# Loads and stores of 512 KB, one for each 128-token tile, in place of 2 MB for each group of 512 tokens

## The chip, the core and the metric

The kernel runs on one core of a Trainium2 chip. Its engines used here: TensorE (PE; its weight loads are shown as PEld), ScalarE (ACT), VectorE (DVE), GpSimd (POOL, only for constants) and SyncE (SP), which issues the loads and stores. All transfers run on the core's 16 DMA engines. The metric is device time in microseconds (us), median of several runs.

## The reference

Each of 64 x 1024 tokens has 1024 features, seen as 16 heads of 64. A product with `route_w` gives 16 logits per token; the head with the largest logit is the token's. Each head has its own 64 x 64 matrix. The output of a token is zero but in its best head, where it is that head's features times that head's matrix.

```python
route_logits = x @ route_w                       # x: 64 x 1024 x 1024, route_w: 1024 x 16
best_head = np.argmax(route_logits, axis=-1)
x_heads = x.reshape(B, S, H, Dh)                 # H = 16, Dh = 64
for h in range(H):
    mask = (best_head == h)
    transformed = np.matmul(x_heads[:, :, h, :], experts[h])
    out[:, :, h, :] = transformed * mask[:, :, None]
```

All is float32; x is 268 MB, and so is the output.

## The kernel before

The 65,536 tokens are cut into 128 groups of 512, and a group into T = 4 tiles of 128 tokens. The program is written out in full, without loops on the chip. `load(g)` (line 83) brings a group with one transfer of 2 MB: partition p gets four tokens that follow each other in memory, 16 KB in one piece, and tile t is the t-th of the four. Four such buffers (`XIN_BUFS`) are 64 KB of each partition, and as much again are the four output buffers.

For each tile, `transpose_tile` turns eight blocks of 128 features by matmuls with the identity (line 93), four to a PSUM buffer, and ACT copies each four to `xt` (line 94). When four tiles are in `xt`, `route` computes the logits of the 512 tokens in 16 matmuls (line 103) in four column strips; ACT copies the result (line 107), four matmuls turn it (line 110), and six DVE instructions (lines 112 to 124) make the mask of 0 and 1. `expert_tile` has 64 small matmuls for a tile (line 133: 8 pairs of heads, two halves of features, two halves of tokens), and DVE multiplies by the mask into `ot` (line 138).

The main loop (line 145) works on two groups at once: the transposes of group g alternate, tile by tile, with the expert matmuls of group g-1. The store of group g-1 (line 157) is one transfer of 2 MB after its fourth tile. In all there are 32 transposes, 256 expert matmuls, 16 + 4 matmuls of the route for a group, 308, and each has a weight load of its own. PE works in order.

SP issues loads and stores from one queue in a fixed order, and an instruction that waits holds all behind it. A load waits until PE has turned the group that used its buffer; a store waits for DVE's fourth multiplication. Transfers signal their end on eight semaphores in turn, and a transfer also waits for the one that used its semaphore before. The expert matrices (`ew`) and `route_w` (`rw`) come once, at the start, in rows of 256 and 64 bytes, issued by ACT.

Of the kernel before, what the change touches and what calls it, by code (L numbers as in the profile page):

```python
# [8 lines left out]
FP32 = mybir.dt.float32  # L9
# [3 lines left out]

P = 128
T = 4
XIN_BUFS = 4
OUT_BUFS = 4
XT_BUFS = 2


@with_exitstack
def kernel(
    ctx: ExitStack,
    tc: tile.TileContext,
    x: bass.AP,
    route_w: bass.AP,
    experts: bass.AP,
    out: bass.AP,
):

    nc = tc.nc
    B, S, D = x.shape
    H = experts.shape[0]
    Dh = D // H  # L40
    N = B * S
    NB = D // P
    G = T * P
    NG = N // G
    CG = 4
    CW = P // CG
    assert D % P == 0 and N % G == 0 and Dh * H == D and 2 * Dh == P and NB % CG == 0

    xg = x.rearrange("b s d -> (b s) d").rearrange("(g p t) d -> g p t d", p=P, t=T)
    og = out.rearrange("b s d -> (b s) d").rearrange("(g p t) d -> g p t d", p=P, t=T)  # L50

    consts = ctx.enter_context(tc.tile_pool(name="consts", bufs=1))
    small = ctx.enter_context(tc.tile_pool(name="small", bufs=2))
    xin_pool = ctx.enter_context(tc.tile_pool(name="xin", bufs=XIN_BUFS))
    xt_pool = ctx.enter_context(tc.tile_pool(name="xt", bufs=XT_BUFS))
    out_pool = ctx.enter_context(tc.tile_pool(name="outp", bufs=OUT_BUFS))
    ps_t_pool = ctx.enter_context(tc.tile_pool(name="ps_t", bufs=2, space=bass.MemoryType.PSUM))
    ps_e_pool = ctx.enter_context(tc.tile_pool(name="ps_e", bufs=2, space=bass.MemoryType.PSUM))
    ps_r_pool = ctx.enter_context(tc.tile_pool(name="ps_r", bufs=1, space=bass.MemoryType.PSUM))
    ps_l_pool = ctx.enter_context(tc.tile_pool(name="ps_l", bufs=1, space=bass.MemoryType.PSUM))  # L60

    ident = consts.tile([P, P], FP32, name="ident")
    make_identity(nc, ident)


    ew = consts.tile([P, NB, Dh], FP32, name="ew")
    ev = experts.rearrange("(p two) d e -> two d p e", two=2)
    for half in range(2):
        nc.scalar.dma_start(out=ew[half * Dh:(half + 1) * Dh, :, :], in_=ev[half])


    rw = consts.tile([P, NB, CW], FP32, name="rw")
    nc.vector.memset(rw, 0.0)  # L73
    with nc.allow_non_contiguous_dma(reason="route_w rows of 64 bytes, once"):
        nc.scalar.dma_start(out=rw[:, :, 0:H], in_=route_w.rearrange("(p k) h -> k p h", k=P))


    rank_i = consts.tile([P, T, H], I32, name="rank_i")
    nc.gpsimd.iota(rank_i, pattern=[[0, T], [-1, H]], base=H, channel_multiplier=0)
    rank = consts.tile([P, T, H], FP32, name="rank")  # L80
    nc.vector.tensor_copy(out=rank, in_=rank_i)  # L81

    def load(g):
        xin = xin_pool.tile([P, T, D], FP32, name="xin", tag="xin")
        nc.sync.dma_start(out=xin, in_=xg[g])
        return xin

    def transpose_tile(xin, xt, t):
        for half in range(2):
            ps_t = ps_t_pool.tile([P, NB // 2, P], FP32, name="ps_t", tag="ps_t")  # L90
            for q in range(NB // 2):
                p = half * (NB // 2) + q
                nc.tensor.transpose(ps_t[:, q, :], xin[:, t, p * P:(p + 1) * P], ident)  # L93
            nc.scalar.copy(  # L94
                out=xt[:, half * (NB // 2):(half + 1) * (NB // 2), t * P:(t + 1) * P],
                in_=ps_t)

    def route(xt):
        ps_r = ps_r_pool.tile([P, G], FP32, name="ps_r", tag="ps_r")
        for r in range(NB // CG):  # L100
            for c in range(CG):
                p = r * CG + c
                nc.tensor.matmul(  # L103
                    ps_r[c * CW:(c + 1) * CW, :], lhsT=rw[:, p, :], rhs=xt[:, p, :],
                    start=(r == 0), stop=(r == NB // CG - 1))
        lgt = small.tile([P, G], FP32, name="lgt", tag="lgt")
        nc.scalar.copy(out=lgt, in_=ps_r)  # L107
        ps_l = ps_l_pool.tile([P, T, P], FP32, name="ps_l", tag="ps_l")
        for t in range(T):
            nc.tensor.transpose(ps_l[:, t, :], lgt[:, t * P:(t + 1) * P], ident)  # L110
        lg = small.tile([P, T, H], FP32, name="lg", tag="lg")
        nc.vector.tensor_reduce(  # L112
            out=lg, in_=ps_l.rearrange("k t (c h) -> k t h c", c=CG)[:, :, 0:H, :],
            op=ALU.add, axis=AX.X)
        mx = small.tile([P, T], FP32, name="mx", tag="mx")
        nc.vector.reduce_max(out=mx, in_=lg, axis=AX.X)  # L116
        hit = small.tile([P, T, H], FP32, name="hit", tag="hit")
        nc.vector.tensor_tensor(  # L118
            out=hit, in0=lg, in1=mx.unsqueeze(2).to_broadcast([P, T, H]), op=ALU.is_ge)
        nc.vector.tensor_tensor(out=hit, in0=hit, in1=rank, op=ALU.mult)  # L120
        top = small.tile([P, T], FP32, name="top", tag="top")
        nc.vector.reduce_max(out=top, in_=hit, axis=AX.X)  # L122
        mask = small.tile([P, T, H], FP32, name="mask", tag="mask")
        nc.vector.tensor_tensor(  # L124
            out=mask, in0=hit, in1=top.unsqueeze(2).to_broadcast([P, T, H]), op=ALU.is_equal)
        return mask

    def expert_tile(xt, mask, ot, t):
        ps_e = ps_e_pool.tile([P, 2, NB, Dh], FP32, name="ps_e", tag="ps_e")
        for p in range(NB):  # L130
            for half in range(2):
                for th in range(2):
                    nc.tensor.matmul(  # L133
                        ps_e[th * 64:(th + 1) * 64, half, p, :],
                        lhsT=xt[half * 64:(half + 1) * 64, p, t * P + th * 64:t * P + (th + 1) * 64],
                        rhs=ew[half * 64:(half + 1) * 64, p, :],
                        start=True, stop=True)
        nc.vector.tensor_tensor(  # L138
            out=ot[:, t, :].rearrange("k (p two e) -> k two p e", two=2, e=Dh),
            in0=ps_e,  # L140
            in1=mask[:, t, :].rearrange("k (p two) -> k two p", two=2).unsqueeze(3).to_broadcast([P, 2, NB, Dh]),
            op=ALU.mult)

    prev = None
    for g in range(NG + 1):
        if g < NG:
            xin = load(g)
            xt = xt_pool.tile([P, NB, G], FP32, name="xt", tag="xt")
        if prev is not None:
            ot = out_pool.tile([P, T, D], FP32, name="ot", tag="ot")  # L150
        for t in range(T):
            if g < NG:
                transpose_tile(xin, xt, t)
            if prev is not None:
                expert_tile(prev[0], prev[1], ot, t)
        if prev is not None:
            nc.sync.dma_start(out=og[g - 1], in_=ot)
        prev = (xt, route(xt)) if g < NG else None


# [28 lines left out]
```

## Time and profile before

| | |
|---|---|
| median of 2 runs | 1873.62 us (1869.89 to 1877.36) |
| profiled execution, its own time | 1866.91 us |
| its span, first to last instruction | 1865.0 us |
| mean granted TensorE clock | 0.926 |
| busy: PE, DVE, ACT | 84%, 44%, 34% |
| HBM read, written | 268.76 MB, 268.44 MB |
| DMA queue of x and out (q1) | 36,864 packets, 76.2% of 16 engines' span |

The page lists, for one execution, how long each engine was busy, which chain of work ended last, and how much each DMA queue moved. "issue" in a chain or a wait is time in which an engine stood still and waited for nothing that the profile shows. A queue's share is the time of its packets over 16 engines' span. The granted clock is 1.00 at 2.4 GHz and 0.50 at 1.2 GHz.

### The profile page before, as it was taken

To read this page: it belongs to the slowest core of one execution; us is meant where nothing else is said; L and a number is where in the kernel's file an instruction comes from. 1 tells how busy PE (TensorE), PEld (TensorE's weight loads), DVE (VectorE), ACT (ScalarE), POOL (GpSimd) and SP (SyncE) were. 2 spreads that over 40 slices of the span, in tenths; PEclk is the share of its full clock that TensorE was granted. 3 is DMA by queue.
4 is the path that set the end of the run, shared out by engine and by line. 5 is a ranking of instruction groups with operands and counts; after the bars stand their busy time and mean duration, and the time that the engine had idled before them with its cause. 6 is when DMAs were issued, how large, how long until landed. Compare 5 with 4: busy or idle time off the path is not lost.

```text
span 1865.0 us, 82352 instructions
## 1 busy us (share of the span) xinstructions
PE 1561.0 (84%) x39424; PEld 1169.3 (63%) x39424; DVE 824.5 (44%) x1282; ACT 640.3 (34%) x1153; POOL 0.8 (0%) x7
## 2 busy tenths in 40 slices
PE   5888888888888888888888888888888888788886
PEld 3666666666666666666666666666666666666565
DVE  1444444444444444444444444434444444444434
ACT  2333333333333333333333333333333333333332
POOL 0000000000000000000000000000000000000000
PEclk8999999899998999998999999988998999999888
DMA  6887887787877787877878877877887877888754
GB/s 238 318 311 273 309 309 289 276 307 294 310 296 286 272 324 280 340 289 273 316 269 302 311 291 281 306 285 273 330 303 275 318 274 294 312 300 308 283 228 183
DMA packets 39294, 542.47 MB, mean 291 GB/s; under 512 B 6192, under 2 KB 6192, under 8 KB 6192
## 3 DMA queue, kind: packets, MB, share of 16 engines
q1 hardware_dynamic: 36864, 536.89, 76.2%
q8 instruction: 308, 5.05, 1.0%
q10 hardware_dynamic: 2096, 0.33, 0.1%
q14 instruction: 26, 0.21, 0.0%
HBM read 268.76 MB, written 268.44 MB: 288 GB/s over the span
## 4 chain that ended last, share of the span: by engine, by line
PE 83%; issue 14%; DMA 1%; ACT 0%; DVE 0%; ACTq 0%
PE ps_e L133 35%; PE ps_t L93 30%; PE ps_r L103 15%; PE ps_l L110 4%; DMA ew<-in_experts_dram 1%; DVE ot L138 0%; ACT xt L94 0%; ACT lgt L107 0%; ACTq L107 0%
## 5 line engine op out<-in xcount | busy, mean ns | idle before, releaser
L138 DVE TENSOR_TENSOR ot<-ps_e,mask 128x1024 f32<-128x1024 f32 x512 | 626.9, 1225 | 683.8 <-PE ps_e L133 673.1
L133 PE MATMUL ps_e<-ew,xt 64*64 64x64 f32 x32768 | 683.0, 231 | 232.1 <-issue 216.6
L94 ACT COPY xt<-ps_t 128x512 f32<-128x512 f32 x1024 | 567.7, 588 | 744.5 <-PE ps_t L93 743.5
L133 PEld LDWEIGHTS ps_e<-ew,xt 64*64 64x64 f32 x32768 | 589.4, 142 | 352.0 <-issue 332.3
L93 PE MATMUL ps_t<-ident,xin 128*128 128x128 f32 x4096 | 621.6, 292 | 62.8 <-issue 53.3
L93 PEld LDWEIGHTS ps_t<-ident,xin 128*128 128x128 f32 x4096 | 472.4, 147 | 206.2 <-issue 177.5
L103 PE MATMUL ps_r<-xt,rw 128*32 128x512 f32 x2048 | 279.6, 666 | 0.0
L107 ACT COPY lgt<-ps_r 128x512 f32<-128x512 f32 x128 | 74.9, 585 | 458.3 <-PE ps_r L103 458.3
L112 DVE TENSOR_REDUCE lg<-ps_l 128x64 f32<-128x256 f32 x128 | 54.3, 424 | 326.5 <-PE ps_l L110 326.5
L103 PEld LDWEIGHTS ps_r<-xt,rw 128*32 128x32 f32 x2048 | 57.6, 117 | 104.6 <-issue 94.2
L110 PE MATMUL ps_l<-ident,lgt 128*128 128x128 f32 x512 | 83.7, 286 | 0.5 <-ACT lgt L107 0.5
L110 PEld LDWEIGHTS ps_l<-ident,lgt 128*128 128x128 f32 x512 | 54.0, 141 | 24.1 <-ACT lgt L107 23.6
L118 DVE TENSOR_TENSOR hit<-lg,mx 128x64 f32<-128x64 f32 x128 | 28.8, 225 | 4.4
L124 DVE TENSOR_TENSOR mask<-hit,top 128x64 f32<-128x64 f32 x128 | 28.8, 225 | 4.4
L120 DVE TENSOR_TENSOR hit<-hit,rank 128x64 f32<-128x64 f32 x128 | 28.8, 225 | 4.4
L116 DVE TENSOR_REDUCE mx<-lg 128x4 f32<-128x64 f32 x128 | 28.2, 220 | 4.4
L122 DVE TENSOR_REDUCE top<-hit 128x4 f32<-128x64 f32 x128 | 28.1, 220 | 4.4
L94 ACT ACT_TABLE_LOAD x1 | 1.3, 1283 | 3.1 <-issue 3.1
L73 DVE MEMSET rw<- 128x256 f32 x1 | 0.3, 272 | 0.9 <-PEq L173 0.9
masks.py:199 POOL TENSOR_SCALAR_AFFINE_SELECT ident<-ident 128x128 f32<-128x128 f32 x1 | 0.3, 292 | 0.0
L81 DVE CAST rank<-rank_i 128x64 f32<-128x64 int32 x1 | 0.3, 264 | 0.1
masks.py:197 POOL MEMSET ident<- 128x128 f32 x1 | 0.2, 204 | 0.3 <-POOLq L173 0.3
(5 smaller groups left out, 0.6 us busy)
## 6 DMA issues: line engine op xcount, KB each, us to landing
xin<-in_x_dram SPq DMA_DIRECT2D x128, 2048.0 KB, 9.0
out_dram<-ot SPq DMA_DIRECT2D x128, 2048.0 KB, 11.6
ew<-in_experts_dram ACTq DMA_DIRECT2D x2, 128.0 KB, 24.2
rw<-in_route_w_dram ACTq DMA_DIRECT2D x1, 64.0 KB, 23.6
```

What stands on the lines that cost most here:

```text
L93: nc.tensor.transpose(ps_t[:, q, :], xin[:, t, p * P:(p + 1) * P], ident)
L94: nc.scalar.copy(out=xt[:, half * (NB // 2):(half + 1) * (NB // 2), t * P:(t + 1) * P], in_=ps_t)
L103: nc.tensor.matmul(ps_r[c * CW:(c + 1) * CW, :], lhsT=rw[:, p, :], rhs=xt[:, p, :], start=(r == 0), stop=(r == NB // CG - 1))
L107: nc.scalar.copy(out=lgt, in_=ps_r)
L110: nc.tensor.transpose(ps_l[:, t, :], lgt[:, t * P:(t + 1) * P], ident)
L112: nc.vector.tensor_reduce(out=lg, in_=ps_l.rearrange("k t (c h) -> k t h c", c=CG)[:, :, 0:H, :], op=ALU.add, axis=AX.X)
L116: nc.vector.reduce_max(out=mx, in_=lg, axis=AX.X)
L118: nc.vector.tensor_tensor(out=hit, in0=lg, in1=mx.unsqueeze(2).to_broadcast([P, T, H]), op=ALU.is_ge)
L120: nc.vector.tensor_tensor(out=hit, in0=hit, in1=rank, op=ALU.mult)
L124: nc.vector.tensor_tensor(out=mask, in0=hit, in1=top.unsqueeze(2).to_broadcast([P, T, H]), op=ALU.is_equal)
L133: nc.tensor.matmul(ps_e[th * 64:(th + 1) * 64, half, p, :], lhsT=xt[half * 64:(half + 1) * 64, p, t * P + th * 64:t * P + (th + 1) * 64], ...
L138: nc.vector.tensor_tensor(out=ot[:, t, :].rearrange("k (p two e) -> k two p e", two=2, e=Dh), in0=ps_e, in1=mask[:, t, :].rearrange("k (p ...
```

## The change

Each tile of 128 tokens becomes a transfer of its own, 512 KB, for loads as for stores. Partition p of tile t now holds one token, 4 KB in one piece, and the 128 tokens of a tile follow each other in memory. There are 20 input buffers and 12 output buffers of 4 KB for each partition (80 and 48 KB). A store is issued after its tile's multiplication. `SPLIT` is 1, so the loop over it runs once and each transpose is as before.

```diff
-XIN_BUFS = 4
-OUT_BUFS = 4
+XIN_BUFS = 20
+OUT_BUFS = 12
 XT_BUFS = 2
+SPLIT = 1
...
-    xg = x.rearrange("b s d -> (b s) d").rearrange("(g p t) d -> g p t d", p=P, t=T)
-    og = out.rearrange("b s d -> (b s) d").rearrange("(g p t) d -> g p t d", p=P, t=T)
+    xg = x.rearrange("b s d -> (b s) d").rearrange("(g t p) d -> g t p d", p=P, t=T)
+    og = out.rearrange("b s d -> (b s) d").rearrange("(g t p) d -> g t p d", p=P, t=T)
...
     def load(g):
-        xin = xin_pool.tile([P, T, D], FP32, name="xin", tag="xin")
-        nc.sync.dma_start(out=xin, in_=xg[g])
-        return xin
+        tiles = []
+        for t in range(T):
+            xin = xin_pool.tile([P, D], FP32, name="xin", tag="xin")
+            nc.sync.dma_start(out=xin, in_=xg[g, t])
+            tiles.append(xin)
+        return tiles
...
-                nc.tensor.transpose(ps_t[:, q, :], xin[:, t, p * P:(p + 1) * P], ident)
+                for c in range(SPLIT):
+                    w = P // SPLIT
+                    nc.tensor.transpose(
+                        ps_t[c * w:(c + 1) * w, q, :],
+                        xin[:, p * P + c * w:p * P + (c + 1) * w], ident)
...
-            out=ot[:, t, :].rearrange("k (p two e) -> k two p e", two=2, e=Dh),
+            out=ot.rearrange("k (p two e) -> k two p e", two=2, e=Dh),
...
-        if prev is not None:
-            ot = out_pool.tile([P, T, D], FP32, name="ot", tag="ot")
         for t in range(T):
             if g < NG:
-                transpose_tile(xin, xt, t)
+                transpose_tile(xin[t], xt, t)
             if prev is not None:
+                ot = out_pool.tile([P, D], FP32, name="ot", tag="ot")
                 expert_tile(prev[0], prev[1], ot, t)
-        if prev is not None:
-            nc.sync.dma_start(out=og[g - 1], in_=ot)
+                nc.sync.dma_start(out=og[g - 1, t], in_=ot)
```

The instructions of PE, ACT, DVE and POOL stay the same in number, kind and order. SP's order changes. At the start of the program SP's queue was this (a name in brackets is what the instruction waits for: DMAHW0 to DMAHW7 are the eight semaphores of transfers):

```order
1 L85 DMA xin<-in_x_dram 128x4096 x4
2 L85 DMA xin<-in_x_dram 128x4096 [waits DMAHW1_49,PE_49]
3 L157 DMA out_dram<-ot 128x4096 [waits DMAHW0_49,DVE_49]
4 L85 DMA xin<-in_x_dram 128x4096 [waits DMAHW4_49,PE_49]
5 L85 DMA xin<-in_x_dram 128x4096 [waits DMAHW5_49,DMAHW2_49,PE_49]
```

and now is this:

```order
1 L88 DMA xin<-in_x_dram 128x1024 x5
2 L88 DMA xin<-in_x_dram 128x1024 [waits DMAHW0_49]
3 L88 DMA xin<-in_x_dram 128x1024 [waits DMAHW1_49]
4 L88 DMA xin<-in_x_dram 128x1024 [waits DMAHW2_49]
5 L88 DMA xin<-in_x_dram 128x1024 [waits DMAHW3_49]
6 L88 DMA xin<-in_x_dram 128x1024 [waits DMAHW4_49]
7 L88 DMA xin<-in_x_dram 128x1024 [waits DMAHW5_49]
8 L88 DMA xin<-in_x_dram 128x1024 [waits DMAHW6_49]
9 L88 DMA xin<-in_x_dram 128x1024 [waits DMAHW7_49]
10 L163 DMA out_dram<-ot 128x1024 [waits DMAHW0_49,DVE_49]
```

Four loads of 2 MB stood ahead of all waits; now five of 512 KB do, and from the sixth on each waits for an earlier transfer to end, 13 of them ahead of the first store. In the middle of the program, SP's queue before:

```order
90 L157 DMA out_dram<-ot 128x4096 [waits DMAHW7_49,DVE_49]
91 L85 DMA xin<-in_x_dram 128x4096 [waits DMAHW0_49,PE_49]
92 L157 DMA out_dram<-ot 128x4096 [waits DMAHW1_49,DVE_49]
93 L85 DMA xin<-in_x_dram 128x4096 [waits DMAHW2_49,PE_49]
94 L157 DMA out_dram<-ot 128x4096 [waits DMAHW3_49,DVE_49]
```

and now:

```order
200 L88 DMA xin<-in_x_dram 128x1024 [waits DMAHW6_49,PE_49]
201 L163 DMA out_dram<-ot 128x1024 [waits DMAHW7_49,DVE_49]
202 L88 DMA xin<-in_x_dram 128x1024 [waits DMAHW0_49,PE_49]
203 L163 DMA out_dram<-ot 128x1024 [waits DMAHW1_49,DVE_49]
204 L163 DMA out_dram<-ot 128x1024 [waits DMAHW2_49,DVE_49]
205 L88 DMA xin<-in_x_dram 128x1024 [waits DMAHW3_49,PE_49]
206 L88 DMA xin<-in_x_dram 128x1024 [waits DMAHW4_49,PE_49]
207 L163 DMA out_dram<-ot 128x1024 [waits DMAHW5_49,DVE_49]
208 L88 DMA xin<-in_x_dram 128x1024 [waits DMAHW6_49,PE_49]
209 L163 DMA out_dram<-ot 128x1024 [waits DMAHW7_49,DVE_49]
```

A load and a store alternated; now the eight transfers of four tiles go load, store, load, two stores, two loads, store, and so on, each behind the transfer that stands eight places ahead of it.

## Rows read from the trace of the kernel before

**Rows 1.** The page's engines: busy us, share of the span, instructions.

```profile
PE 1561.0 (84%) x39424; PEld 1169.3 (63%) x39424; DVE 824.5 (44%) x1282; ACT 640.3 (34%) x1153; POOL 0.8 (0%) x7
```

**Rows 2.** The chain that ended last, by engine, share of the span.

```profile
PE 83%; issue 14%; DMA 1%; ACT 0%; DVE 0%; ACTq 0%
```

**Rows 3.** Waits of PE: us in total, times, longest us.

```profile
PE ps_e L133 <- issue: 216.6, 137, 3.9
PE ps_t L93 <- issue: 53.3, 21, 3.6
PE ps_e L133 <- DMA ew<-in_experts_dram: 13.6, 1, 13.6
PE ps_t L93 <- DMA xin<-in_x_dram: 8.7, 1, 8.7
```

**Rows 4.** DMA queues: packets, MB, share of 16 engines' span.

```profile
q1 hardware_dynamic: 36864, 536.89, 76.2%
q8 instruction: 308, 5.05, 1.0%
q10 hardware_dynamic: 2096, 0.33, 0.1%
```

**Rows 5.** Timeline of PE: start us, us, line, operation, shape, count, [idle before].

```profile
185.26 1.35 PE L133 MATMUL ps_e<-ew,xt 64*64 64x64 f32 x59 [1.73 <-issue]
186.54 1.97 PE L93 MATMUL ps_t<-ident,xin 128*128 128x128 f32 x8
188.44 1.60 PE L133 MATMUL ps_e<-ew,xt 64*64 64x64 f32 x64
189.97 1.92 PE L103 MATMUL ps_r<-xt,rw 128*32 128x512 f32 x16
191.82 0.88 PE L93 MATMUL ps_t<-ident,xin 128*128 128x128 f32 x6
192.66 0.66 PE L110 MATMUL ps_l<-ident,lgt 128*128 128x128 f32 x4
193.15 0.38 PE L93 MATMUL ps_t<-ident,xin 128*128 128x128 f32 x2
193.46 1.16 PE L133 MATMUL ps_e<-ew,xt 64*64 64x64 f32 x64
194.55 1.09 PE L93 MATMUL ps_t<-ident,xin 128*128 128x128 f32 x8
195.58 1.16 PE L133 MATMUL ps_e<-ew,xt 64*64 64x64 f32 x64
196.67 1.09 PE L93 MATMUL ps_t<-ident,xin 128*128 128x128 f32 x8
197.69 1.16 PE L133 MATMUL ps_e<-ew,xt 64*64 64x64 f32 x64
198.78 1.09 PE L93 MATMUL ps_t<-ident,xin 128*128 128x128 f32 x8
199.81 0.34 PE L133 MATMUL ps_e<-ew,xt 64*64 64x64 f32 x8
201.97 1.04 PE L133 MATMUL ps_e<-ew,xt 64*64 64x64 f32 x56 [1.82 <-issue]
```

**Rows 6.** Windows: us, busy of five engines, granted clock, DMA share, GB/s (last three).

```profile
185.30:189.97 4.67, 4.67 (x131) 4.16 (x132) 1.22 (x1) 1.17 (x2) 0.00 (x0) 0.63 0.35 84
196.10:202.10 6.00, 4.18 (x141) 3.61 (x137) 2.72 (x3) 2.37 (x5) 0.00 (x0) 1.00 0.98 380
197.00:200.00 3.00, 3.00 (x87) 2.60 (x86) 2.11 (x2) 1.60 (x4) 0.00 (x0) 1.00 1.01 426
189.40:191.40 2.00, 2.00 (x56) 0.92 (x48) 1.22 (x1) 0.00 (x0) 0.00 (x0) 0.99 1.02 254
3.00:23.00 20.00, 2.88 (x12) 2.28 (x12) 0.00 (x0) 3.04 (x4) 0.00 (x0) 0.81 1.00 403
```

**Rows 7.** Timeline of PE: the first and the last route of the program.

```profile
32.69 1.92 PE L103 MATMUL ps_r<-xt,rw 128*32 128x512 f32 x16
1843.56 1.92 PE L103 MATMUL ps_r<-xt,rw 128*32 128x512 f32 x16
```

## The prediction

> **What bounds the kernel now.** I read the page's table of engines first. TensorE (PE) is busy 84% of the span, with 39,424 matmuls and as many weight loads [rows 1], and the chain that ended last is PE for 83% and "issue" for 14% [rows 2]: PE alone sets the end, and a seventh of the time it stands still with nothing that the profile names to wait for. The table of waits sizes it: 216.6 + 53.3 = 269.9 us in 158 stops, 1.71 us each [rows 3].
>
> What those stops are, I take from two views together. The queue "instruction" moved 308 packets, 5.05 MB, so 16.4 KB each [rows 4]; 2 x 39,424 / 308 = 256 instructions, thus one packet for 128 matmuls with their weight loads. PE's timeline between two stops holds 59+8+64+16+6+4+2+64+8+64+8+64+8+8 = 383 matmuls, within one record of 3 x 128 [rows 5]: PE stops only where a block of 256 instructions ends. In that stretch the first block ran while the DMA engines were 0.35 busy, and no stop followed; the third ran while they were 0.98 busy, and PE then stood for 1.82 us [rows 5, 6]. So I read the stops as PE waiting for its own code, whose packet shares the 16 DMA engines with x and out, in packets of 16 KB. Of 308 crossings 158 show as a stop.
>
> "Runtime: NRT & Kernel Launch" of the Trainium skill (Instruction fetch mechanics) also has code come in 16 KiB blocks, but calls the cost of the crossing "mostly hidden". The trace disagrees, with stops at half the crossings. By that rule the 270 us would have another cause and would stay, which is the second rival.
>
> The engine time of DMA is the second limit: q1 was busy 76.2% of 1865 us, 1421 us per engine [rows 4]. A kernel that gets much faster meets it.
>
> **The change, part by part.** PE, ACT and DVE run the same instructions in the same order. What changes is the transfers.
>
> *PE's floor.* Between the routes a group takes, at full clock and without stops, 193.46-189.97 = 3.49, then 199.81-193.46 = 6.35, and a last expert block of 194.55-193.46 = 1.09: 10.95 us with rounding [rows 5]. First route at 32.69, 127 periods, and 1865.0-1843.56 = 21.4 behind the last one [rows 7]: 32.7 + 1391 + 21.4 = 1445 us. The span has 420 us more: 270 are stops, and 150 the rest, above all half clock right behind them (eight transposes 1.97 instead of 1.09 us [rows 5]; 0.63 granted against 1.00 [rows 6]).
>
> *Start.* Four 2 MB loads lie ahead of the small expert rows, and PE waits 13.6 us for those [rows 3]. With packets a quarter the size the expert rows get their turns sooner: 0 to 13.6 us gained, I take 8. The earlier first tile gains nothing, since PE would wait for the expert weights anyway. *End.* The last store is 512 KB: at most 1.5 MB at 426 GB/s [rows 6], 0 to 3.7 us; I take 3.
>
> *The stops.* 128 matmuls at 72 per 2.11 us take 3.75 us, so a code packet that stopped PE took 3.75 + 1.71 = 5.5 us on average. Its part that has nothing to do with other data lies between its own duration, 1.0% of 16 engines over 308 packets = 0.97 us [rows 4], and 4.7 us (the first block, after which no stop came). If the wait is for a number of data packets, it falls to a quarter: the fetch takes between 0.97 + 1.1 = 2.1 us, hidden, and 4.7 + 0.2 = 4.9 us, which leaves 1.15 us. What remains is 0 to 182 us over 158 fetches; I take 0.3 us each, 47, near the lower end because the 4.7 us block was half at the low clock and shows only that nothing was left to wait for. Of the 150 us I leave a third, 50 (0 to 150). PE's limit is then 1445 - 8 - 3 + 47 + 50 = 1531 us.
>
> *DMA.* The best stretch of three microseconds moved 426 GB/s with all engines busy [rows 6]; 536.89 MB at that rate are 1260 us. The other 161 of the 1421 us are 0.63 us for each of 256 transfers; one place where they fall is the start of a load, where full engines moved 254 GB/s, whereas loads right behind each other kept 403 even with the small rows among them [rows 6]. After the change there are 1024 transfers, 131,072 data packets and 16 completion packets for each transfer (36,864 now is 256 x 144), together 147,456: 6,912 more for each engine. A small packet took 0.1% of the engines' time over 2,096, 14 ns (7 to 21 by rounding) [rows 4]: +97 us (48 to 145). For the 161 us, the lower end is no growth (the bytes set it); by the number of changes of direction, six in eight transfers in SP's new order, 768 against 256, it is 484; by transfers 645. I take 240, nearer the low end, because many loads now start on idle engines, which a fuller queue avoids. Code packets: 298 us, 19 if spread over 16 engines, all 298 if one carries them; I take 19. And 10 us at both ends without overlap. Sum: 1260 + 97 + 240 + 19 + 10 = **1626 us**.
>
> *At no cost, with their cover.* SP issues 1024 transfers instead of 256; it has nothing else to do, and a load that stands behind a store's wait on DVE is covered by 20 tiles in stock, five groups of 11 us. Each transfer waits for the one eight before it: 4 MB under way, 9.8 us of work at 426 GB/s, enough to keep the engines fed. If that cover goes, PE's wait for xin, 8.7 us once now [rows 3], comes back in each group.
>
> DMA's 1626 lies above PE's 1531, so the DMA engines end last: 1626 us of span. The profiled run took 1866.9 for a span of 1865.0, and the median shown is 6.7 above that: **1635 us**, own range 1565 to 1720 (161 instead of 240; 320, half of the price by transfers). What is late next is then a load, seen by PE.
>
> **The rivals.**
> *PE stays the limit* (the 0.63 us scales with the bytes or hides): 1531 + 9 = 1540. For it: a third of the engines' loss lies at idle starts that vanish; against: the two limits are only 95 us apart and PE would need the engines 95% busy.
> *The stops don't shrink*, because a code packet waits for a fixed amount of data rather than of packets, or because they aren't fetches: only start and end are gained, 1865 - 11 + 9 = 1863. For it: the trace has one packet size, so it can't tell number from bytes. Against: the fetch that found the engines 0.98 busy would, at the same bytes, find only 512 KB transfers, which are through four times sooner.
> *Slower: each transfer pays its own start.* If the 0.63 us belongs to the transfer, 1024 of them cost 645 us: 1260 + 97 + 645 + 19 + 10 + 9 = 2040. It decides from 0.50 us each, (1911 - 1395) / 1024. For it: the 254 GB/s at the start of a load; against: 403 in a row of four. "DMA: Bandwidth & Descriptors" of the Trainium skill (Rules for kernel authors) asks for at least 1 MiB in a transfer for full bandwidth, which speaks for this rival; its fit of 2.0 us and the bytes at 436 GB/s would by my estimate make 3.3 ms of 1024 transfers if none overlapped. The row of loads back to back shows that they overlap.
> *In between*, 0.32 to 0.43 us for each transfer: 1720 to 1836. If one engine carried all code packets, it would add up to 279 us to the forecast (1914); its chance is in the cases of no change and slower.
>
> **How the numbers follow.** Forecast 0.38, PE the limit 0.28, in between 0.11: together 0.77 for faster by over 2% (under 1836; 2% is about what a measurement of this kernel can tell). Stops that don't shrink, or DMA that eats the gain just up: 0.11 within 2%. Each transfer's own start: 0.12 slower (over 1911). The range 1520 to 1860 leaves out the slow case, half of the unchanged one's upper part and a little below PE's 1540, some 0.2.
>
> **What would show it.** PE's waits for "issue" under 100 us and a mean granted clock above 0.95 bear out the step on code; at 200 us and more it fails. q1 above 90% of the engines, with waits of PE for xin of 50 us and more, bear out that DMA ends last; no such wait and q1 at 85% mean the first rival. A q1 above 95% in a span of 1900 us or more is the slow case. If the code packets' own mean rises from 0.97 us far above 2, my price for a fetch among small packets is wrong.

## The result, and the profile after

The changed kernel takes 1749.01 us (1743.95 to 1754.08) against 1873.62: a ratio of 0.9335, 95% interval 0.9194 to 0.9476. The forecast was 1635 and the range 1520 to 1860. The profiled execution has a span of 1752.3 us, 112.7 less than before.

First the rows of the page, the engines and the DMA queues, which answer to [rows 1, 4]:

```profile
PE 1517.8 (87%) x39424; PEld 1132.8 (65%) x39424; DVE 824.7 (47%) x1282; ACT 638.2 (36%) x1153; POOL 0.8 (0%) x7
q1 hardware_dynamic: 147456, 536.94, 86.8%
q8 instruction: 310, 5.08, 1.2%
```

Then PE's waits (us in total, times, longest), which answer to [rows 3]:

```profile
PE ps_e L141 <- issue: 155.2, 121, 4.0
PE ps_t L99 <- issue: 36.9, 25, 2.8
PE ps_r L111 <- issue: 20.8, 14, 3.3
PE ps_t L99 <- DMA xin<-in_x_dram: 4.5, 2, 4.4
PE ps_l L118 <- issue: 3.8, 3, 2.3
PE ps_e L141 <- DMA ew<-in_experts_dram: 2.5, 1, 2.5
```

The stops are still there: 155.2 + 36.9 + 20.8 + 3.8 = 216.7 us in 163 stops, against 269.9 in 158: as many, but each shorter, 1.33 us on average for 1.71. PE waits for x no more than 4.5 us, at the start. Set side by side, the two spans differ by three rows: stops 53.2 us less, PE's busy time 43.2 less (1561.0 against 1517.8, the same instructions), and the waits for the first x and for the expert weights 15.3 less (22.3 against 7.0). That is 111.7 of the 112.7 us.

The traces also hold the time of every DMA packet, those of the queue "instruction" among them, and they tie the stops to code. In the kernel before, 152 of the 159 stops over 0.25 us end 1.1 to 1.65 us after a code packet has ended, and 154 of 159 in the changed kernel, with a median of 1.4 us in both. In the 128 matmuls before such a stop just one code packet starts (157 and 159 of 159). And 155 of the 158 distances between neighbouring stops of the kernel before are a multiple of 128 matmuls, or one short of it. So a stop ends when the block of code that was fetched during the block before it has come.

PE's busy time falls because its clock is up more often. Windows of both kernels (the first is of before; the last three columns are the granted clock, the DMA share and GB/s):

```profile
60.00:1800.00 1740.00, 1478.06 (x37396) 1107.86 (x37389) 781.78 (x1217) 606.84 (x1094) 0.00 (x0) 0.93 0.79 295
```

```profile
60.00:1700.00 1640.00, 1425.30 (x37105) 1064.75 (x37104) 775.88 (x1208) 598.72 (x1084) 0.00 (x0) 0.96 0.89 312
1703.81:1736.59 32.78, 32.78 (x931) 25.08 (x925) 19.32 (x30) 14.85 (x27) 0.00 (x0) 1.00 0.49 196
```

The last row is the end of the changed kernel, where all loads have landed and only stores run, at half the DMA share. PE's timeline there shows the first and last of four routes:

```profile
1703.81 1.92 PE L111 MATMUL ps_r<-xt,rw 128*32 128x512 f32 x16
...
1736.59 1.92 PE L111 MATMUL ps_r<-xt,rw 128*32 128x512 f32 x16
```

Three groups in 32.78 us, 10.93 each, with PE busy throughout and the clock at 1.00. Without loads beside it, the program runs at the floor that the prediction worked out, and no block of code is late.

### The profile page after: what moved, and what is told of

It reads as the page before. It is cut to its first block, busy times and chain, and to the rows that moved or that the text cites. A ratio compares the mean times of both kernels' runs of the same rounds, so it can differ in the third digit from the quotient of the medians.

```text
span 1752.3 us, 84634 instructions
## 1 busy us (share of the span) xinstructions
PE 1517.8 (87%) x39424; PEld 1132.8 (65%) x39424; DVE 824.7 (47%) x1282; ACT 638.2 (36%) x1153; POOL 0.8 (0%) x7
## 3 DMA queue, kind: packets, MB, share of 16 engines
q1 hardware_dynamic: 147456, 536.94, 86.8%
## 4 chain that ended last, share of the span: by engine, by line
PE 86%; issue 12%; DMA 1%; DVE 0%; ACT 0%; ACTq 0%
PE ps_e L141 35%; PE ps_t L99 31%; PE ps_r L111 15%; PE ps_l L118 4%; DMA ew<-in_experts_dram 1%; DVE ot L146 0%; ACT lgt L115 0%; ACTq L70 0%; ACT xt L102 0%; ACTq L115 0%
## 5 line engine op out<-in xcount | busy, mean ns | idle before, releaser
L141 PE MATMUL ps_e<-ew,xt 64*64 64x64 f32 x32768 | 658.0, 226 | 159.9 <-issue 155.2
L141 PEld LDWEIGHTS ps_e<-ew,xt 64*64 64x64 f32 x32768 | 566.8, 138 | 271.6 <-issue 263.3
L99 PE MATMUL ps_t<-ident,xin 128*128 128x128 f32 x4096 | 604.2, 286 | 42.5 <-issue 36.9
L99 PEld LDWEIGHTS ps_t<-ident,xin 128*128 128x128 f32 x4096 | 458.3, 144 | 186.7 <-issue 159.6
L111 PE MATMUL ps_r<-xt,rw 128*32 128x512 f32 x2048 | 279.2, 642 | 20.8 <-issue 20.8
```

The costliest lines, as they stand in the source:

```text
L99: nc.tensor.transpose(ps_t[c * w:(c + 1) * w, q, :], xin[:, p * P + c * w:p * P + (c + 1) * w], ident)
L111: nc.tensor.matmul(ps_r[c * CW:(c + 1) * CW, :], lhsT=rw[:, p, :], rhs=xt[:, p, :], start=(r == 0), stop=(r == NB // CG - 1))
L141: nc.tensor.matmul(ps_e[th * 64:(th + 1) * 64, half, p, :], lhsT=xt[half * 64:(half + 1) * 64, p, t * P + th * 64:t * P + (th + 1) * 64], ...
```

## The experiments

Each kernel is compared with runs of the kernel before on the same chip, whose medians were 1869 to 1871 us. "Stops" is the sum of PE's waits for "issue" in the one profiled execution of a kernel. Single runs of the kernel before lay between 1860 and 1886 us, so small differences in stops between two kernels say nothing.

### The size of the packets alone

The kernel before with only the order of the tokens changed. It keeps its four-plus-four buffers and 2 MB transfers, now in packets of 4 KB:

```diff
-... .rearrange("(g p t) d -> g p t d", p=P, t=T)
+... .rearrange("(g t p) d -> g p t d", p=P, t=T)
```

Expected: 

> The kernel before with one part of the change alone: 2 MB transfers and 4 buffers as before, but tile t now holds tokens in the changed order, so that every transfer has 512 packets of 4 KB instead of 128 of 16 KB. Theory N (a code packet waits for a number of data packets): the stops of PE fall below the 217 us of the changed kernel, to 100 us or less, and the time to 1700 us or less. Theory Q (a code packet waits for the amount of data that is queued on its engine, up to a limit of some tens of KB): the queue is as deep as before, the stops stay at 250 to 280 us and the time at 1850 to 1880 us; the gain then came from the size and spacing of the transfers.

Measured: 1889.66 us, ratio 1.0079 (1.0040 to 1.0118). The queues and the waits of this kernel:

```profile
q1 hardware_dynamic: 135168, 536.89, 78.9%
PE ps_e L133 <- issue: 247.1, 145, 3.8
PE ps_t L93 <- issue: 51.7, 25, 4.1
```

Packets of a quarter the size, and 298.8 us of stops in place of 269.9. Theory N, on which the forecast stood, falls; stops and time lie a little above what theory Q had. So the change doesn't gain by its packets. What is left is that its transfers are smaller, that each is handed over as its tile is ready, and that the stock is deeper. The packet time is 0.789 x 1898.0 = 1497 us for each engine against 1421: 98,304 packets more, 6,144 on each engine, at 12 ns each.

### Without loads, without stores

The changed kernel with the first group's x for all groups; and with the stores of the last group alone:

```diff
-            xin = load(g)
+            xin = load(g) if g == 0 else xin0
+            xin0 = xin
```

Expected: 

> The changed kernel without the loads behind the first group (every group works on the first one's x, so the output is that group's, again and again). Engines of DMA then carry only stores, half the bytes. N and Q: the queue is empty at most fetches, stops under 30 us, time 1420 to 1470 us, the period of a group 10.9 us. If the stops have nothing to do with data transfers: 217 us of stops stay and the time is 1720 to 1750.

```diff
-                nc.sync.dma_start(out=og[g - 1, t], in_=ot)
+                if g == NG:
+                    nc.sync.dma_start(out=og[g - 1, t], in_=ot)
```

Expected: 

> The changed kernel without the stores of all groups but the last. Loads of 512 KB come at the pace at which PE frees their buffers. Q: a load is 1.3 us of work on each engine in some 2.8 us, so a fetch waits at most that long: stops under 40 us, time 1430 to 1480. N: likewise few. [...]

Measured: 1429.53 us with stores alone (0.7617, 0.7577 to 0.7658) and 1477.42 with loads alone (0.7880, 0.7834 to 0.7926). q1, the stops and the engines with stores alone:

```profile
q1 hardware_dynamic: 74304, 270.57, 46.7%
PE ps_e L141 <- issue: 2.7, 6, 0.8
PE ps_r L111 <- issue: 0.2, 1, 0.2
PE 1413.6 (99%) x39424; PEld 1077.7 (75%) x39424; DVE 824.3 (58%) x1282; ACT 635.8 (44%) x1153; POOL 0.8 (0%) x7
```

and with loads alone:

```profile
q1 hardware_dynamic: 74304, 270.57, 54.9%
PE ps_e L141 <- issue: 22.5, 44, 1.8
PE ps_r L111 <- issue: 3.2, 4, 2.1
```

PE's instructions are the same, and so are the blocks of code. With half the data beside them the stops go from 216.7 us to 2.9 and 25.7. So they are made by the data transfers, and mostly by loads and stores together.

### Half the expert instructions

The changed kernel with both token halves in one matmul. (The program has 32 expert matmuls for a tile; each of them leaves two records, hence the 64 of the timeline, and so do the route's eight with their 16 records. A transpose leaves one.)

```diff
-                for th in range(2):
-                    nc.tensor.matmul(
-                        ps_e[th * 64:(th + 1) * 64, half, p, :],
-                        lhsT=xt[half * 64:(half + 1) * 64, p, t * P + th * 64:t * P + (th + 1) * 64],
+                nc.tensor.matmul(
+                    ps_e[:, half, p, :],
+                    lhsT=xt[half * 64:(half + 1) * 64, p, t * P:(t + 1) * P],
```

Expected: 

> The changed kernel with the two token halves of each expert product in one matmul (128 columns of weights instead of 64): half the expert instructions, 180 for 308 matmul records in a group, so a block of 256 instructions lasts some 7.8 us instead of 4.7. Code fetches take 4 to 7 us, so N and Q both give stops under 40 us if PE's time for the expert products stays, and the time then meets the DMA engines, 1521 us of packet time and what they cannot overlap: 1540 to 1620 us. If the wider matmul costs PE more (two of them at a time instead of four), up to 130 us come back: 1650 to 1700. If the stops are not code fetches, they stay at 200 us and more.

Measured: 1851.75 us, 0.9867 (0.9807 to 0.9926). The page's rows of this kernel (its engines, the queues of data and of code, the expert matmuls with busy us, mean ns, idle before):

```profile
PE 1837.6 (99%) x23040; PEld 1505.0 (81%) x23040; DVE 824.4 (45%) x1282; ACT 635.5 (34%) x1153; POOL 0.8 (0%) x7
q1 hardware_dynamic: 147456, 536.94, 82.7%
q8 instruction: 182, 2.98, 0.7%
L140 PE MATMUL ps_e<-ew,xt 64*128 64x64 f32 x16384 | 1028.3, 275 | 1.6 <-DMA ew<-in_experts_dram 1.5
```

and the same matmuls in the changed kernel:

```profile
L141 PE MATMUL ps_e<-ew,xt 64*64 64x64 f32 x32768 | 658.0, 226 | 159.9 <-issue 155.2
```

No wait for "issue" is left, although the same data move on engines that are 82.7% busy: the wide matmuls leave 182 code packets, and a block lasts 1850 / 182 = 10.2 us on average, longer than its fetch. With the times of the code packets above, this settles what the stops are. As a version it loses: the expert products take 1028 us instead of 658, more than the stops and the low clock cost. I had expected at most 130 us there.

### The size of the transfers

Loads alone at 2 MB, the kernel before without the stores of all groups but the last:

Expected: 

> The kernel before (2 MB, 16 KB packets) without the stores of all groups but the last. To be set beside the 512 KB kernel with loads alone, which took 1477 us with 26 us of stops: the same bytes, the same pace. Theory Q: a load of 2 MB fills each engine's queue for some 5 us of every 11, so a third or more of the fetches meet a queue: stops 60 to 150 us, time 1520 to 1640. Theory U: the engines are as idle as there, stops about 26 us, time 1470 to 1495.

Measured: 1522.38 us (0.8129, 0.8100 to 0.8159). Its waits:

```profile
PE ps_e L133 <- issue: 29.6, 49, 1.6
PE ps_e L133 <- DMA ew<-in_experts_dram: 13.3, 1, 13.3
PE ps_t L93 <- issue: 8.6, 11, 1.6
PE ps_r L103 <- issue: 0.6, 1, 0.6
```

38.8 us of stops against 25.7 with 512 KB. Between the two profiled spans (1513.5 and 1476.4) lie 37.1 us, and 15.5 of these are the slower start: 22.0 us of waits for the first x and the expert weights against 6.5. Bundling loads alone makes few stops, fewer than theory Q had it and more than theory U.

Two tiles to a transfer, 1 MB, once in packets of 4 KB and once, with two neighbouring tokens in a partition, of 8 KB:

```diff
-XIN_BUFS = 20
-OUT_BUFS = 12
+XIN_BUFS = 10
+OUT_BUFS = 6
...
-... .rearrange("(g t p) d -> g t p d", p=P, t=T)
+... .rearrange("(g u t p) d -> g u p t d", p=P, u=2, t=2)    # 8 KB: "(g u p t) d -> g u p t d"
...
+        for u in range(2):
+            xin = xin_pool.tile([P, 2, D], FP32, name="xin", tag="xin")
+            nc.sync.dma_start(out=xin, in_=xg[g, u])
```

Expected, 4 KB: 

> The changed kernel with 1 MB transfers, two tiles in each (10 input and 6 output buffers of two tiles, the same memory); packets stay 4 KB. Theory Q (a code packet waits for the data queued ahead of it on its engine, so the size and spacing of transfers count): between the kernels, stops of PE 235 to 280 us, time 1790 to 1850 us. Theory U (only the share of engine time that data takes counts, not how it is bundled): like the changed kernel, 217 us of stops and 1735 to 1765.

Expected, 8 KB: 

> The kernel with 1 MB transfers, with two neighbouring tokens in a partition, so 8 KB packets in place of 4 KB. B: bundles as with 1 MB and 4 KB packets, stops 170 to 195 us, time 1700 to 1735. E: half the packets, packet time under 1445 us (some 1400), stops 140 to 180 us, time 1670 to 1710.

And each tile's transfer cut in two, 256 KB in packets of 2 KB:

```diff
-            nc.sync.dma_start(out=xin, in_=xg[g, t])
+            for c in range(2):
+                nc.sync.dma_start(out=xin[:, c * 512:(c + 1) * 512], in_=xg[g, t][:, c * 512:(c + 1) * 512])
```

Expected: 

> The changed kernel with each tile's transfers cut in two, 256 KB in packets of 2 KB. E: packets and transfers double, packet time 1600 us and more, stops 230 to 300 us, time 1780 to 1900. B alone: smaller bundles, stops under 217 us, time under 1740.

Measured: 1 MB of 4 KB 1720.48 us (0.9202, 0.9144 to 0.9260); 1 MB of 8 KB 1757.53 (0.9397, 0.9355 to 0.9440); 256 KB 1720.26 (0.9164, 0.9109 to 0.9219). q1 and the waits for "issue" of the 1 MB kernel with 4 KB packets:

```profile
q1 hardware_dynamic: 139264, 536.90, 84.6%
PE ps_e L141 <- issue: 146.7, 108, 4.0
PE ps_r L111 <- issue: 20.0, 12, 3.9
PE ps_t L99 <- issue: 18.6, 15, 2.5
PE ps_l L118 <- issue: 0.2, 1, 0.2
```

and of the 256 KB kernel:

```profile
q1 hardware_dynamic: 294912, 537.00, 90.1%
PE ps_e L142 <- issue: 157.5, 144, 4.0
PE ps_t L100 <- issue: 19.8, 19, 2.0
PE ps_r L112 <- issue: 16.4, 14, 2.1
```

| transfer, packet | time | stops | packet time on q1, per engine |
|---|---|---|---|
| 2 MB, 16 KB (before) | 1874 | 269.9 | 1421 |
| 2 MB, 4 KB | 1890 | 298.8 | 1497 |
| 1 MB, 8 KB | 1758 | 199.4 | 1417 |
| 1 MB, 4 KB | 1720 | 185.5 | 1445 |
| 512 KB, 4 KB (the change) | 1749 | 216.7 | 1521 |
| 256 KB, 2 KB | 1720 | 193.7 | 1555 |

The step lies between 2 MB and 1 MB, with packets the same: 298.8 to 185.5 us of stops. Below it the stops lie between 185 and 217, and neither size nor packet time orders them; theories Q and U both missed the 1 MB kernel of 4 KB packets, B and E that of 8 KB. Theory U (share of engine time alone) falls with the first step: 2 MB and 512 KB need about the same time on the engines, 1497 and 1521 us, and differ by 82 us of stops. Theory E, its successor, falls with the last row: the most packet time and nearly the fewest stops. Of theory Q only the coarse part stands, that a group's load and store handed over whole make the most stops. The 1 MB kernel of 4 KB packets and the 256 KB kernel have the lowest medians, below the change's, but the intervals of both overlap with the change's.

The packet records show what the wait of a code packet goes with. Take the start of each block of code, the data of loads and stores that SP has issued by then and no engine has begun, and the time until the next code packet starts. In the kernel before that time is 1.1 us on average with less than 0.5 MB ahead (77 blocks) and 3.8 us with 1.5 MB and more (180 blocks). With 2 MB transfers in 4 KB packets it is 1.2 and 3.6 us (71 and 207 blocks): the wait goes with the amount of data ahead, and a quarter of the packet size changes nothing. In the changed kernel, too, it rises, from 1.2 to 3.9 us, and 1.5 MB lie ahead at 12% of the blocks instead of 59%. But the mean over all blocks is 2.8 us in both kernels, since with 0.5 to 1.5 MB ahead the changed kernel waits longer (3.0 us against 2.1). So how smaller transfers take 53 us off the stops isn't shown by this.

### Handed over four at a time

Transfers of 512 KB in packets of 4 KB, four together, each over 32 partitions, for loads and stores alike, with the four-plus-four buffers of 2 MB of the kernel before:

```diff
+            for c in range(4):
+                nc.sync.dma_start(out=xin[c * 32:(c + 1) * 32, :, :], in_=xg[g, c * 32:(c + 1) * 32])
```

Expected: 

> Transfers of 512 KB in packets of 4 KB as in the changed kernel, but handed over four at a time: a group's four loads (32 partitions each) go out together when its buffer is free, and its four stores together after the fourth tile. Theory B (what counts is how many bytes are handed to the engines at once): stops of PE back at 260 to 300 us, time 1850 to 1900 us, although the transfers are small. Theory E (what counts is the time that the engines need for the transfers): q1 near the changed kernel's 1521 us of packet time, stops near 217, time 1740 to 1780.

Measured: 2745.34 us, 1.4671 (1.4625 to 1.4717). q1 and PE's longest waits:

```profile
q1 hardware_dynamic: 147456, 536.94, 84.3%
PE ps_t L94 <- DMA xin<-in_x_dram: 371.8, 66, 15.1
PE ps_e L134 <- issue: 231.4, 104, 5.0
```

It says nothing on bundling. The same 147,456 packets took 0.843 x 2749.1 = 2317 us for each engine instead of 1521, and PE waited for x. The kernel with 2 MB transfers in 4 KB packets hands over the same data at the same places over 128 partitions, and took 1497: here the cut by partitions made the transfers slow.

### The stock, and another issuer

The changed kernel with 8 and 6 buffers in place of 20 and 12:

Expected: 

> The changed kernel with 8 input and 6 output buffers of one tile in place of 20 and 12. If the stock is not what the gain rests on (Q and U both): 1735 to 1770 us, waits of PE for x under 20 us. If loads need the five groups of stock because they are late at times: waits of PE for x of 50 us and more, and the time above 1790.

Measured: 1779.57 us, 0.9546 (0.9480 to 0.9613), with 227.5 us of stops and 4.9 us of waits for x. The interval begins where the change's ends (0.9476): the deep stock may be worth about two per cent, but not because loads were late. It isn't what the gain rests on in the main: with fewer tiles in stock than the kernel before (8 and 6 for 16 and 16), this kernel keeps two thirds of it.

The changed kernel with `nc.gpsimd.dma_start` for the loads, and the same for the 1 MB kernel with 8 KB packets:

Expected: 

> The changed kernel with the loads issued by GpSimd, so that loads and stores come from two queues. Q, if the data queue that counts is the engine's as a whole: stops 170 to 230 us, time 1710 to 1770. If the wait is in SP's queue alone, which now has half the data: stops under 70 us, time 1500 to 1600. If GpSimd's way of issuing is dearer for the engines: PE waits for x, or the time is above 1800.

Expected, 1 MB: 

> 1 MB transfers of 8 KB packets, loads issued by GpSimd as in the kernel with loads from GpSimd, which was some 1% faster than the changed kernel. B and E both: 0 to 1.5% below the kernel with 1 MB transfers of 8 KB packets, 1655 to 1710 us, stops 120 to 180 us.

Measured: 1732.91 us, 0.9273 (0.9228 to 0.9318), stops 195.6; and 1810.49, 0.9668 (0.9635 to 0.9702), stops 225.2. In two queues the stops stay, so the wait isn't in SP's queue alone. For 1 MB it is slower than from SP (1757.53), against what both theories had.

## Why the prediction was right in the time and wrong in the step

*What the stops are: right.* They come with the blocks of code: they end 1.4 us after a code packet does, are gone when a block holds more work (the halved expert instructions), and nearly gone when data are thinned out (stores alone). The rival by which they aren't fetches is ruled out. The Trainium skill's "mostly hidden" ("Runtime: NRT & Kernel Launch", Instruction fetch mechanics) holds with stores alone, 2.9 us of 1430; with loads and stores on the engines it doesn't.

*"If the wait is for a number of data packets, it falls to a quarter": the step that failed.* From it came 47 us of stops left; measured are 216.7, above the 200 that I had named as the sign of failure, though the mean clock did pass 0.95. The kernel with 2 MB transfers of 4 KB packets shows it directly: smaller packets alone leave 298.8. The time until a code packet starts is 2.8 us on average before and after, and goes with the amount of data ahead of it. The packets' own duration, which I had as a price at risk, hardly rose: 1.2% of 16 x 1752.3 us over 310 packets is 1.09 us, from 0.97. The Trainium skill, "DMA: Bandwidth & Descriptors" (Queues, rings and completion order), has an engine take turns between its queues at the end of a packet, which there is a bundle of typically 9 to 17 descriptors. The profile doesn't show whether its packets of 16 and 4 KB are such bundles, so no run here can test that rule. The rival in which the wait goes by the amount of data was nearer, but I let it end in no gain, since I read "amount" as unchanged. In fact smaller transfers took 53 us off the stops. Why is open: the table above isn't ordered by the size of packet or transfer, or by packet time, and the run meant to separate bundling from transfer size did not.

*That the DMA engines end last: wrong.* Packet time was 0.868 x 1752.3 = 1521 us for each engine, close to the 1597 of the sum without code and ends, but PE waited for x only 4.5 us and loads were never late again. By the sign that I gave, PE stays the limit, as in the first rival, whose 1540 fails by the same stops. The engines' load comes back through the code instead, which has no stock beyond one block: its packet is fetched while the block before it runs.

*The price of a transfer: too high, on the safe side.* The forecast let the 161 us that it spread over transfers grow by 79, to 240 for 1024 of them; the slow rival by 484. 4 KB packets alone brought packet time from 1421 to 1497, and the change, with 768 transfers more and their completion packets, stands only 24 above those 1497; 1 MB transfers of 4 KB packets even stand 52 below them. So most of the 161 us belong to something else than the number of transfers. The price of a packet, 14 ns by the rounded row, was 12 between the two 2 MB kernels and 7 between the two 1 MB kernels (1445 - 1417 us over 4,096 packets for each engine): no constant.

*Start: mechanism right, a part left out.* 8 us forecast, 15.3 measured. The first route comes at 17.39 instead of 32.69; with 2 MB transfers in 4 KB packets it comes at 26.27, so the smaller packets, which the 8 us stood for, gave 6.4. The first line is of before, the second of that kernel, the others of the changed kernel:

```profile
25.16 0.47 PE L133 MATMUL ps_e<-ew,xt 64*64 64x64 f32 x2 [13.55 <-DMA ew<-in_experts_dram]
26.27 2.61 PE L103 MATMUL ps_r<-xt,rw 128*32 128x512 f32 x16 [1.83 <-DMA rw<-in_route_w_dram]
11.18 0.47 PE L141 MATMUL ps_e<-ew,xt 64*64 64x64 f32 x2 [2.50 <-DMA ew<-in_experts_dram]
...
17.39 3.64 PE L111 MATMUL ps_r<-xt,rw 128*32 128x512 f32 x16
```

The expert weights arrive before 11.2 us instead of 25.2. The rest of the 15.3 came with the smaller transfers; the earlier first tile, which I had at nothing, took 4.2 us off the wait for x alone. The floor was right: 1445 - 8 - 3 = 1434 us without stops, and stores alone took a span of 1430.4.

*The low clock: mechanism right, size with the stops.* I left 50 of the 150 us. PE's busy time for the same instructions is 1413.6 us with stores alone, 147.4 more before and 104.2 more after: 0.55 and 0.48 us for each us of stop, at granted clocks of 0.926 and 0.962 on average against 0.999 with stores alone. The whole price of a stop follows from the spans. Take 1430.4 us as the span without stops. What each kernel with all its data is above that, set against its stops: before 434.6 / 269.9 = 1.61, the change 321.9 / 216.7 = 1.49, 2 MB of 4 KB 1.56, 1 MB 1.50 and 1.62, 256 KB 1.53, the small stock 1.50, GpSimd 1.52 and 1.64. In these nine kernels one microsecond of stop goes with 1.5 to 1.6 us of span, start and end included. With loads alone, where stops are few, it is more: 46.0 / 25.7 = 1.79 with 512 KB.

With the two measured terms the forecast's own sum for PE comes out: 1445 - 8 - 3 + 217 + 104 = 1755 us, against a span of 1752.3. It was short by 170 us of stops and 54 of low clock, and the limit of the DMA engines, from which the 1635 came, never applied.

So that 1749 lies in the range is luck in part: it lies in the case "in between" that I gave 0.11, whose price is for transfers, and it came another way, by PE and its code.

## What to carry to other kernels

Where PE stops for "issue", count instructions between two stops (a matmul record and its weight load are two): multiples of 256 mean that code is late. Here it helped to have less data on the DMA engines at the time, and fewer instructions for the same work took all stops away, but only pay if the larger instructions aren't slower, as they were here. Loads with stock hid a DMA share of 87%; code had one block of stock and didn't. Count each such stop at about one and a half times its length.

## What the runs showed of the hardware

- With blocks of code of 4.6 us on average without stops (1413.6 / 308), PE hardly stopped for code with the DMA engines 47 to 55% busy by data (2.9 and 25.7 us), and 217 us at 87%. With blocks of 10.2 us it didn't stop at 83%.
- PE went on 1.4 us (median) after the end of a code packet, which itself took 1.0 to 1.1 us; the packet started 1.1 us after the block before it began with under 0.5 MB of data ahead, and 3.8 us with 1.5 MB and more (the kernel before).
- 512 KB transfers over 32 partitions, four handed over together, moved 197 GB/s over the whole span, where 512 KB transfers over 128 partitions moved 310, as the page has it for the two kernels (and 2 MB ones in the same packets 286):

```profile
DMA packets 149895, 542.61 MB, mean 197 GB/s; under 512 B 18480, under 2 KB 18480, under 8 KB 149552
```

```profile
DMA packets 149903, 542.68 MB, mean 310 GB/s; under 512 B 18480, under 2 KB 18480, under 8 KB 149552
```

- Transfers of 256 KB, 2 KB for a partition, cost the engines only 9% more packet time than 2 MB with 16 KB (1555 against 1421 us), and the kernel was no slower for it than with 1 MB.
